# The feed-forward part of two token chunks computed with seven block products in place of eight

## Chip, cores and metric

One core of a Trainium2 chip runs the whole kernel. The metric is the device time of one execution in microseconds (us); lower is better.

## What is computed

A trunk layer over 1152 tokens (128 context tokens and 1024 latent tokens), width D = 1024: four mixers, an output projection, a gated feed-forward part with a width-3 convolution, and a final norm. What the change touches is the last stretch:

```
h = rmsnorm(x, p['norm2_g']) * (1.0 + sc2) + sh2
z = h @ p['ffn_w_up']                      # 1024 -> 2 x 2816
zc = conv_w[0] * z[t-1] + conv_w[1] * z[t] + conv_w[2] * z[t+1] + conv_b
a, b = jnp.split(zc, 2, axis=-1)           # in rows of 64 tokens (latent)
x = x + g2 * ((gelu(a) * b) @ p['ffn_w_down'])   # 2816 -> 1024
y = rmsnorm(x, final_norm_g)
```

Everything is float32.

## The kernel before

Activations lie transposed: features on the 128 partitions, tokens along the free side, in three chunks c = 0, 1, 2 of 384 tokens (`CH`). Chunk 0 holds the 128 context tokens and 256 latent ones, chunks 1 and 2 latent tokens alone. A float32 product is made of three matmuls on split operands (`mm3`, L216): each weight tile and each activation tile is held as a rounded part (`hi`) and the rest (`lo`), and hi·hi, hi·lo and lo·hi are added up in PSUM (L219 to L221). Splitting costs a cast on ScalarE (ACT) and a subtraction on VectorE (DVE) or GpSimd (POOL): `load_split` (L201) does it for weights of 128x1024 with the subtraction on POOL (L213), `put_hl` (L269) for activations.

The order of the instructions on TensorE (PE) and on the SP queue, which issues nearly all loads, is that of the program; the other engines' orders are laid out by the compiler's scheduler, each engine then running its list strictly in order. Buffers are tiles of pools with a fixed number of slots: three raw weight tiles, four `whi`/`wlo` pairs, eight PSUM banks (three `psg`, five `psx`). A load waits for its slot.

The output projection (`wout`, L1412) adds its products to the residual `acc[c]` in SBUF (`acc_add`, L1393), takes squares on ACT (L1429), and `norm2` (L1448) makes from them the normed and split input `h2[c]` of the feed-forward part: sums over partitions on PE (`stats`, L223, L229), a root on ACT and a reciprocal on DVE, a broadcast by PE (`bcast`, L256, L266), then `ada_apply` (L283; L289 on DVE, L278 and L294 on ACT, L275 and L279 for the `lo` parts).

The feed-forward part (`ffn`, L1533) goes over 22 column blocks f of 128. `ffn_up` (L1487) loads the block's weights for a and for b and does for each chunk 8 x 3 matmuls each (`gemm`, L556), the convolution (`conv`, L1456: L1459 on ACT, two or four instructions L1461 on DVE), the gelu (L1472, ACT) and the product with b (L1480, POOL), and splits the result g (L1483, L1484); g never leaves SBUF. After every second block `ffn_down` (L1507) multiplies the two g tiles of each chunk by two row blocks of w_down, 8 output blocks of 6 matmuls each, and adds each onto `acc` (L1396, DVE). The first two blocks are interleaved by chunk (`ffn_up2`, L1493), so that the norm of chunk 2 has its place between the matmuls of chunks 0 and 1. The last `ffn_down` takes squares (L1519) and runs `final` (L1542) for each chunk: sums on PE (L1548), broadcast (L266), output tiles on DVE (L1565) and POOL (L1563), stores from the SP queue (L1566).

In all the feed-forward part has 22 x 3 x 48 = 3168 matmuls up and 22 x 3 x 24 = 1584 down, each of a 128x128 weight and 384 columns.

## Time and profile before

| what | us |
|---|---|
| time, median of 3 runs (lowest, highest) | 1466.95 (1464.58, 1469.35) |
| the profiled execution, its own time | 1465.13 |
| its span in the trace | 1463.2 |
| PE busy | 1400.9 (96%) |
| DVE, POOL, ACT busy | 744.8, 531.5, 506.8 |

The span is what the profiler saw, from the first to the last instruction; the time of the same execution is 1.9 us longer. A matmul's busy time overlaps that of its neighbours, so the pace of matmuls is read from how many start in a stretch.

### The profile page before, as it was taken

The page shows a single profiled execution, that of the slowest core. Times are in us where ns is not written, and L with a number is a line of the kernel's source. Part 1 is how long each engine was busy: PE and PEld are TensorE (multiplying, and loading weights), DVE is VectorE, ACT ScalarE, POOL GpSimd, SP SyncE. Part 2 cuts the span into 40 slices and gives each one's busy share as a digit, 9 for nine tenths or more (in the row PEclk, how much of TensorE's full clock was granted, in tenths as well). Part 3 has the DMA queues.
Part 4 walks back from the last instruction along what each step waited for, and adds up shares of the span by engine and source line. Part 5 has one row for each costly group of instructions (what it writes and reads, how often), then busy time and mean ns, then how long its engine had stood idle before and what let it go on. Part 6 is the DMA issues. An engine that isn't in the chain of part 4 may idle for free.

```text
span 1463.2 us, 24504 instructions
## 1 busy us (share of the span) xinstructions
PE 1400.9 (96%) x9852; PEld 1330.1 (91%) x9852; DVE 744.8 (51%) x1571; ACT 506.8 (35%) x910; POOL 531.5 (36%) x500
## 2 busy tenths in 40 slices
PE   5999989898999999999999999999999999999996
PEld 2898778776898799999999999999999999999996
DVE  7797464544756411654444444535353535353545
ACT  6533212445456321653231313131313131313134
POOL 2243696644415233633231313132322222223224
...
GB/s 346 158 147 260 277 215 231 127 179 123 100 166 149 221 22 37 58 30 58 44 44 42 33 43 44 43 44 44 43 44 44 30 46 28 57 30 58 15 1 129
DMA packets 167602, 139.36 MB, mean 95 GB/s; under 512 B 19393, under 2 KB 156993, under 8 KB 167489
## 3 DMA queue, kind: packets, MB, share of 16 engines
...
## 4 chain that ended last, share of the span: by engine, by line
PE 78%; DMA 6%; POOL 5%; DVE 5%; issue 3%; ACT 2%; ACTq 0%; SPq 0%; POOLq 0%; DVEq 0%
PE psg L219 17%; PE psg L220 17%; PE psg L221 17%; PE psx L219 6%; PE psx L221 6%; PE psx L220 6%; DMA gv_s<-t_ev 1%; PE psx L229 1%; DMA raw<-w_in 1%; DMA raw<-w_ada 1%; PE psx L746 1%; PE psx L266 1%; POOL wlo L213 1%; DVE Gt L1323 1%; PE psg L593 1%
## 5 line engine op out<-in xcount | busy, mean ns | idle before, releaser
L219 PE MATMUL psg<-hm,whi 128*128 128x384 f32 x1560 | 538.6, 345 | 1.3 <-ACT hm L278 1.3
L220 PE MATMUL psg<-hm,whi 128*128 128x384 f32 x1560 | 530.4, 340 | 2.7 <-POOL hm L275 2.7
L221 PE MATMUL psg<-hm,wlo 128*128 128x384 f32 x1560 | 529.7, 340 | 1.1 <-POOL wlo L213 1.1
L213 POOL TENSOR_TENSOR wlo<-raw,whi 128x1024 fp32r<-128x1024 f32 x88 | 223.3, 2544 | 458.8 <-ACT whi L209 458.8
L219 PEld LDWEIGHTS psg<-hm,whi 128*128 128x128 f32 x1560 | 295.2, 189 | 10.6 <-issue 7.7
L220 PEld LDWEIGHTS psg<-hm,whi 128*128 128x128 f32 x1560 | 295.2, 189 | 4.8 <-POOL hm L275 3.4
L221 PEld LDWEIGHTS psg<-hm,wlo 128*128 128x128 f32 x1560 | 295.2, 189 | 1.4 <-POOL wlo L213 1.4
L1396 DVE SCALAR_TENSOR_TENSOR acc<-psx,mod,acc 128x384 f32<-128x384 f32 (+1 forms) x352 | 170.5, 514 | 83.3 <-PE psx L221 83.2
L209 ACT CAST whi<-raw 128x1024 fp32r<-128x1024 f32 x92 | 95.4, 1049 | 263.1 <-PE psx L220 193.9
L219 PE MATMUL psx<-ghi,whi 128*128 128x384 f32 x528 | 177.7, 337 | 0.0
L220 PE MATMUL psx<-glo,whi 128*128 128x384 f32 x528 | 177.4, 336 | 0.0
L221 PE MATMUL psx<-ghi,wlo 128*128 128x384 f32 x528 | 177.3, 336 | 0.0
L1461 DVE SCALAR_TENSOR_TENSOR t_ga<-psg,vecs,t_ga 128x378 f32<-128x378 f32 (+1 forms) x176 | 88.2, 511 | 170.5 <-ACT t_ga L1459 167.3
L1461 DVE SCALAR_TENSOR_TENSOR t_gb<-psg,vecs,t_gb 128x378 f32<-128x378 f32 (+1 forms) x176 | 87.9, 510 | 75.3 <-ACT t_gb L1459 72.6
L1480 POOL TENSOR_TENSOR t_gb<-t_gb,t_ga 128x384 f32<-128x384 f32 x66 | 67.5, 1022 | 150.1 <-DVE t_gb L1461 144.3
L219 PEld LDWEIGHTS psx<-ghi,whi 128*128 128x128 f32 x528 | 100.0, 189 | 0.0
L220 PEld LDWEIGHTS psx<-glo,whi 128*128 128x128 f32 x528 | 99.8, 189 | 0.0
L221 PEld LDWEIGHTS psx<-ghi,wlo 128*128 128x128 f32 x528 | 99.8, 189 | 0.0
L1483 ACT CAST ghi<-t_gb 128x384 fp32r<-128x384 f32 x66 | 33.9, 513 | 180.9 <-POOL t_gb L1480 180.9
L1484 DVE TENSOR_TENSOR glo<-t_gb,ghi 128x384 fp32r<-128x384 f32 x66 | 36.9, 559 | 109.6 <-ACT ghi L1483 109.6
L1472 ACT ACTIVATE t_ga<-t_ga 128x384 f32<-128x384 f32 x66 | 34.7, 526 | 95.4 <-DVE t_ga L1461 95.4
L1459 ACT ACTIVATE t_ga<-psg,vecs 128x384 f32<-128x384 f32 x66 | 44.2, 670 | 50.8 <-PE psg L221 50.8
...
## 6 DMA issues: line engine op xcount, KB each, us to landing
...
```

Source lines behind the costliest of these rows:

```text
L209: nc.scalar.copy(hi[:, :w], raw[:, :w])
L213: e.tensor_tensor(out=lo[:, :w], in0=raw[:, :w], in1=hi[:, :w].bitcast(F32), op=ALU.subtract)
L219: nc.tensor.matmul(ps, wh, ah, start=first and k == 0, stop=False)
L220: nc.tensor.matmul(ps, wh, al, start=False, stop=False)
L221: nc.tensor.matmul(ps, wl, ah, start=False, stop=last and k == nk - 1)
L1396: self.nc.vector.scalar_tensor_tensor(out=x, in0=ps[:, s0:s1], scalar=self.mod[:, sect + m, j:j + 1], in1=x, op0=ALU.mult, op1=ALU.add)
L1459: nc.scalar.activation(t, ps, AF.Identity, bias=self.vec("cb", f, 1), scale=w(1))
L1461: stt = lambda o, i, j: V.scalar_tensor_tensor(out=o, in0=i, scalar=w(j), in1=o, op0=ALU.mult, op1=ALU.add)
L1472: self.nc.scalar.activation(t, t, AF.Gelu_apprx_tanh)
L1480: G.tensor_tensor(out=t, in0=t, in1=ga, op=ALU.mult)
L1483: nc.scalar.copy(hi, t)
L1484: V.tensor_tensor(out=lo, in0=t, in1=hi.bitcast(F32), op=ALU.subtract)
```

## The change

Chunks 1 and 2 (768 tokens) together are treated as a product of 2x2 block matrices by a form of Strassen's scheme. Up: the four quarters of the input are features 0-511 and 512-1023 of chunk 1 and of chunk 2; the four quarters of the weights for one f are the two feature halves of its a block and of its b block. Seven products of sums of quarters (`hB[1]` to `hB[7]` with a, b and the sums P and Q), of 4 x 3 matmuls each, take the place of eight. Chunk 0 is computed as before. Down: the quarters are rows 0-1407 and 1408-2815 of w_down by its two column halves, and g of blocks f < 11 and f >= 11 by chunk; seven products of 11 x 4 x 3 matmuls take the place of eight.

The pieces, by the names in the diff:

- `wout` also writes each piece of the residual `acc` to DRAM (`x_s`), from the ACT queue. `norm2(2)` and `h_sums` now come ahead of the feed-forward part; `h_sums` makes the sums of quarters in place in `acc[1]` and `acc[2]` and splits them. The pool `zb`, opened by `open_zb`, lies where these two `acc` tiles were, and holds the weight sums (tag S), the g tiles and others.
- `ffn_up` handles one f at a time: per f on PE p1 (12 matmuls), three (36), a for chunk 0 (24), p2 (12), p43 (24), b for chunk 0 (24). `up_w` loads and sums weights; a and Q are split with DVE, b and P with POOL. `up_tail` finishes the outputs of chunks 1 and 2. `store` writes g to DRAM (`GV_s`; `G0_s` for chunk 0), for f >= 11 with four differences made on POOL (`tsub`), all by the ACT queue.
- `ffn_down` runs after all of up: first chunk 0 in all eight PSUM banks (22 steps of 24 matmuls), while the sums of w_down are made (S1 to S4 in SBUF), then the products 1, 6, 2, 7, 5, 4, 3, each in four banks (11 steps of 12 matmuls). g is loaded from DRAM and split again, step by step (`gload`); products 1, 2 and 4 load quarters of w_down again. The residual comes back by `xin` into two slots, and `final` of chunks 0 and 1 runs inside products 1 and 3.

```diff
                     def f(ps):
                         self.acc_add(c, m, ps, 16)
+                        self.nc.scalar.dma_start(self.x_s[c, :, m], self.acc[c][:, m])
...
-    def norm2(self, c, pool):
-        r = self.stats(self.sqs[c], 3, 1.0 / D, pool)
+    def norm2(self, c, zs):
+        r = self.stats(self.sqs[c], 3, 1.0 / D, zs)
         yield
         xs = [self.acc[c][:, i] for i in range(KT)]
         pb = self.bcast(r, 3)
-        self.h2.append(self.ada_apply(xs, c, self.A2, self.mod[:, 24:32, :], pool, pb))
+        if c == 0:
+            self.h2 = self.ada_apply(xs, c, self.A2, self.mod[:, 24:32, :], self.shared, pb)
+            yield
+            return
+        for k in (0, 4, 1, 5, 2, 6, 3, 7):
+            self.nc.vector.scalar_tensor_tensor(out=xs[k], in0=xs[k], scalar=self.A2[:, k, 1:2], in1=pb, op0=ALU.mult, op1=ALU.mult)
+            self.nc.scalar.activation(xs[k], xs[k], AF.Identity, bias=self.mod[:, 24 + k, 1:2])
+        if c == 1:
+            self.hB = {v: [None] * 4 for v in range(1, 8)}
+            for k in range(4):
+                self.hB[1][k] = self.put_hl(1, xs[k])
+                self.hB[2][k] = self.put_hl(1, xs[k + 4], None, "pool")
         yield
+    def h_sums(self, ext):
+        V = self.nc.vector
+        ex = lambda: ext.tile([P, CH], F32R, tag="e", name="he", bufs=24)
...
+        for k in range(4):
+            b11, b21 = self.acc[1][:, k], self.acc[1][:, k + 4]
+            b12, b22 = self.acc[2][:, k], self.acc[2][:, k + 4]
+            self.hB[3][k] = split(b22, (self.hm(2), self.hm(2)), G)
+            tt(b11, b12, b11)
+            tt(b12, b22, b12)
+            tt(b22, b22, b11)
+            tt(b21, b21, b22)
+            self.hB[6][k] = split(b22, (ex(), ex()), V)
+            self.hB[7][k] = split(b12, (ex(), ex()), G)
+            self.hB[5][k] = split(b11, (self.hm(2), self.hm(2)), V)
+            self.hB[4][k] = split(b21, (ex(), ex()), G)
...
+        def sums():
+            p = sp().tile([P, 1024], F32, tag="S", name="s24", bufs=2)
+            q = sp().tile([P, 1024], F32, tag="S", name="s31", bufs=2)
+            V.tensor_tensor(out=q[:, hi], in0=b[:, lo], in1=b[:, hi], op=ALU.add)
+            V.tensor_tensor(out=q[:, lo], in0=a[:, lo], in1=b[:, lo], op=ALU.subtract)
+            V.tensor_tensor(out=p[:, lo], in0=q[:, hi], in1=a[:, lo], op=ALU.subtract)
+            V.tensor_tensor(out=p[:, hi], in0=a[:, hi], in1=p[:, lo], op=ALU.subtract)
+            return p, q
+        return lambda: split(a, V), lambda: split(b, G), sums, split
...
+    def mmq(self, ps, w, o, v, first=True):
+        for i in range(4):
+            x = slice(o + i * P, o + (i + 1) * P)
+            self.mm3(ps, (w[0][:, x], w[1][:, x]), self.hB[v][i], i, 4, first, True, not first)
...
+    def zt(self, tag):
+        pool, n = {"p1": ("zs", 2), "X": ("zs", 2), "T": ("zs", 2), "gb": ("zb", 7), "Y": ("zb", 1), "c": ("zb", 2)}[tag]
+        return getattr(self, pool).tile([P, CH], F32, tag=tag, name="z" + tag, bufs=n)
...
+    def up_tail(self, f, ps, ga, X, Y, C22):
+        tt = lambda o, x, y: self.nc.vector.tensor_tensor(out=o, in0=x, in1=y, op=ALU.add)
+        self.gs[f, 2] = [C22, None]
+        c21 = self.zt("c")
+        tt(c21, ps[7], X)
+        g1 = self.up_gb(c21, 1, f, ga[1])
+        c12 = self.zt("c")
+        tt(c12, ps[5], X)
+        ga[2] = self.up_ga(c12, 2, f)
+        g2 = self.up_gb(C22, 2, f, ga[2])
+        self.store(f, g1, g2)
...
+    def store(self, f, g1, g2):
...
+        put = lambda v, t: nc.scalar.dma_start(self.GV_s[v - 1, f % 11], t)
+        if f < 11:
+            put(1, g1)
+            self.gk = g1, g2
+            return
+        b11, b12 = self.gk
+        put(2, g1)
+        put(3, g2)
+        T = lambda x, y: self.tsub(x, y)
+        t1 = T(b12, b11)
+        put(5, t1)
+        t3 = T(g2, b12)
+        put(7, t3)
+        t2 = T(g2, t1)
+        put(6, t2)
+        put(4, T(g1, t2))
+
+    def tsub(self, x, y):
+        t = self.zt("T")
+        self.nc.gpsimd.tensor_tensor(out=t, in0=x, in1=y, op=ALU.subtract)
+        return t
...
+        fs = [f for j in range(11) for f in (j, j + 11)]
...
+        def p1(f, w):
+            x[f] = {1: self.psx(CH)}
+            self.mmq(x[f][1], w, 0, 1)
+            t = st[f] = self.zt("p1")
+            nc.scalar.copy(t, x[f][1])
+
+        def p2(f, w):
+            self.mmq(x[f][1], w, 512, 2, False)
+            return self.up_ga(x[f].pop(1), 1, f)
+
+        def three(f, p, q):
+            X = self.zt("X")
+            ps = self.psx(CH)
+            self.mmq(ps, p, 0, 6)
+            tt(X, ps, st.pop(f))
+            x[f][7] = self.psx(CH)
+            self.mmq(x[f][7], q, 0, 7)
+            Y = self.zt("Y")
+            tt(Y, x[f][7], X)
+            x[f][5] = self.psx(CH)
+            self.mmq(x[f][5], q, 512, 5)
+            tt(Y, x[f][5], Y)
+            return X, Y
+
+        def p43(f, b, p):
+            self.mmq(x[f][7], b, 512, 4, False)
+            self.mmq(x[f][5], p, 512, 3, False)
...
+        f, g = fs[0], fs[1]
+        wa, wb, sums, split = self.up_w(f, sp)
...
+        a, b = wa(), wb()
+        p1(f, a)
+        ga[f][0] = self.up_ga(self.gemm(a, self.h2), 0, f)
+        ga[f][1] = p2(f, a)
+        wa2, wb2, sums2, split = self.up_w(g, sp)
+        nb = self.gemm(b, self.h2)
+        a2 = wa2()
+        p1(g, a2)
+        ga[g][0] = self.up_ga(self.gemm(a2, self.h2), 0, g)
+        ga[g][1] = p2(g, a2)
+        self.open_zb()
+        self.up_gb(nb, 0, f, ga[f][0])
+        P_, Q_ = sums()
+        q, p = split(Q_, V), split(P_, nc.gpsimd)
+        X, Y = three(f, p, q)
+        p43(f, b, p)
+        self.up_tail(f, x[f], ga[f], X, None, Y)
+        P_, Q_ = sums2()
+        b2 = wb2()
+        q, p = split(Q_, V), split(P_, nc.gpsimd)
+        X, Y = three(g, p, q)
+        nb = self.gemm(b2, self.h2)
+        p43(g, b2, p)
+        self.up_gb(nb, 0, g, ga[g][0])
...
+        for f in fs[2:]:
+            wa, wb, sums, split = self.up_w(f, sp)
+            ga = {}
+            a = wa()
+            P_, Q_ = sums()
+            q, p = split(Q_, V), split(P_, nc.gpsimd)
+            b = wb()
+            p1(f, a)
+            X, Y = three(f, p, q)
+            ga[0] = self.up_ga(self.gemm(a, self.h2), 0, f)
+            ga[1] = p2(f, a)
+            p43(f, b, p)
+            nb = self.gemm(b, self.h2)
+            self.up_gb(nb, 0, f, ga[0])
+            self.up_tail(f, x[f], ga, X, None, Y)
...
+        def gload(src, e):
+            r = dn.tile([P, CH], F32, tag="gr", name="gr", bufs=3)
+            nc.sync.dma_start(r, src)
+            h = dn.tile([P, CH], F32R, tag="gh", name="gh", bufs=4)
+            l = dn.tile([P, CH], F32R, tag="gl", name="gl", bufs=4)
+            nc.scalar.copy(h, r)
+            e.tensor_tensor(out=l, in0=r, in1=h.bitcast(F32), op=ALU.subtract)
+            return h, l
+
+        g0 = [gload(self.G0_s[f], G) for f in (0, 11)]
...
+        def fin(c, m, src):
+            for s0, s1, j in SEG[c]:
+                t = acc[c][:, m, s0:s1]
+                V.scalar_tensor_tensor(out=t, in0=src[:, s0:s1], scalar=self.mod[:, 40 + m, j:j + 1], in1=t, op0=ALU.mult, op1=ALU.add)
+            q = dn.tile([P, CH], F32, tag="sq", name="sq", bufs=2) if sq.get(c) else dn.tile([P, CH], F32, tag="ss", name="ss", bufs=2)
+            nc.scalar.activation(q, acc[c][:, m], AF.Square)
+            if sq.get(c):
+                G.tensor_tensor(out=sq[c], in0=sq[c], in1=q, op=ALU.add)
+            else:
+                sq[c] = q
+        sq = {}
...
+            for i in range(KT):
+                y = dn.tile([P, CH], F32, tag="yo", name="yo", bufs=4)
+                V.scalar_tensor_tensor(out=y, in0=xs[i], scalar=self.vec("nf", i, 1), in1=pb, op0=ALU.mult, op1=ALU.mult)
+                nc.sync.dma_start(self.a["o_y"][i * P:(i + 1) * P, c * CH:(c + 1) * CH], y)
+            yield
...
+        def stream(nk, steps, ps, first, late=3, side=()):
+
+            n = len(ps)
+            held, side = [], dict(side)
+            for i, mk in enumerate(steps):
+                hi, lo, o, g = mk()
+                if i >= nk - late:
+                    held.append((i, hi, lo, o, g))
+                    continue
+                for m in range(n):
+                    x = slice(o + m * P, o + (m + 1) * P)
+                    self.mm3(ps[m], (hi[:, x], lo[:, x]), g, i, nk, first, True, not first)
+                if i in side:
+                    side[i]()
+            for m in range(n):
+                for i, hi, lo, o, g in held:
+                    x = slice(o + m * P, o + (m + 1) * P)
+                    self.mm3(ps[m], (hi[:, x], lo[:, x]), g, i, nk, first, True, not first)
+                yield m
...
+                    s1, s2, s3, s4 = s
+                    V.tensor_tensor(out=s1, in0=ra[:, hi], in1=rb[:, hi], op=ALU.add)
+                    V.tensor_tensor(out=s3, in0=ra[:, lo], in1=ra[:, hi], op=ALU.subtract)
+                    V.tensor_tensor(out=s2, in0=s1, in1=ra[:, lo], op=ALU.subtract)
+                    V.tensor_tensor(out=s4, in0=rb[:, lo], in1=s2, op=ALU.subtract)
+                    return h, l, 0, g
...
+                        hl[k // 2] = wsplit(x, n * 512, V if k % 4 else G)
+                    h, l = hl[k // 2]
+                    return h, l, k % 2 * 512, gload(self.GV_s[v - 1, k], V if k % 2 else G)
+                yield mk
+        A_, B_ = B[0:4], B[4:8]
+        for m in stream(22, n0_steps(), B, True, 3, {6: lambda: xin(0)}):
+            fin(0, m, B[m])
+        f0 = final(0, (B_[0], B_[1]))
+        xin(1)
+        for m in stream(11, p_steps(1, (0, 0)), A_, True, 1, {4: lambda: next(f0), 7: lambda: next(f0)}):
+            nc.scalar.copy(X[:, m], A_[m])
+        next(f0)
+        for m in stream(11, p_steps(6, 2), B_, True, 1):
+            tt(X[:, m], B_[m], X[:, m])
+        xin(2)
+        for m in stream(11, p_steps(2, (11, 0)), A_, False, 1):
+            fin(1, m, A_[m])
+        for m in stream(11, p_steps(7, 3), B_, True, 1):
+            tt(Y[:, m], B_[m], X[:, m])
+        for m in stream(11, p_steps(5, 1), A_, True, 1):
+            tt(Y[:, m], A_[m], Y[:, m])
+            fin(2, m + 4, Y[:, m])
+        for m in stream(11, p_steps(4, (11, 512)), B_, False, 1):
+            tt(Y[:, m], B_[m], X[:, m])
+            fin(1, m + 4, Y[:, m])
+        f1 = final(1, (B_[0], B_[1]))
+        for m in stream(11, p_steps(3, 4), A_, False, 3, {4: lambda: next(f1), 7: lambda: next(f1)}):
+            tt(X[:, m], A_[m], X[:, m])
+            fin(2, m, X[:, m])
+        next(f1)
+        for _ in final(2, (B_[2], B_[3])):
+            pass
...
+        n = k.norm2(2, k.zs)
+        next(n), next(n)
         L.close()
-        ff = k.ffp = L.open("ff")
-        L.close(4)
-        R.close()
+        k.h_sums(L.open("ext"))
+
+        def open_zb():
+            R.close()
+            k.zb = R.open("zb")
+        k.open_zb = open_zb
+        k.ffn_up()
+        L.close(2)
+        R.close(3)
+        k.ffn_down(L.open("dn"))
+        L.close(2)
```

## Rows read from the trace of the kernel before

**Rows 1.** The page: span, busy time and chain shares by engine.
```profile
span 1463.2 us, 24504 instructions
...
PE 1400.9 (96%) x9852; PEld 1330.1 (91%) x9852; DVE 744.8 (51%) x1571; ACT 506.8 (35%) x910; POOL 531.5 (36%) x500
...
PE 78%; DMA 6%; POOL 5%; DVE 5%; issue 3%; ACT 2%; ACTq 0%; SPq 0%; POOLq 0%; DVEq 0%
```
**Rows 2.** Windows: stretch, us, busy (and count) by engine, PE clock, DMA share, GB/s.
```profile
700.00:800.00 100.00, 100.00 (x574) 100.00 (x573) 43.94 (x87) 25.97 (x38) 25.58 (x15) 1.00 0.15 43
...
1427.90:1449.80 21.90, 19.94 (x103) 18.97 (x102) 15.18 (x29) 13.96 (x28) 10.93 (x12) 0.84 0.26 95
1435.00:1440.00 5.00, 5.00 (x23) 5.00 (x22) 4.25 (x8) 3.31 (x7) 2.74 (x3) 0.72 0.77 281
```
**Rows 3.** Timeline (start, us, instruction), TensorE, last token chunk.
```profile
1427.57 0.34 PE L221 MATMUL psx<-ghi,wlo 128*128 128x384 f32 x1
1428.82 0.83 PE L1548 MATMUL psg<-ones,t_sq 128*128 128x1 f32 x6 [0.92 <-POOL t_sq L1524]
...
1431.60 1.65 PE L266 MATMUL psg<-ident,r 128*128 128x128 f32 x6 [0.79 <-DVE r L238]
...
1434.00 0.52 PE L219 MATMUL psx<-ghi,whi 128*128 128x384 f32 x1
1434.32 0.52 PE L220 MATMUL psx<-glo,whi 128*128 128x384 f32 x1
...
1449.45 0.34 PE L221 MATMUL psx<-ghi,wlo 128*128 128x384 f32 x1
```
**Rows 4.** Timeline, all engines, end of the output projection, up to 612 us.
```profile
596.63 1.39 PE L229 MATMUL psx<-ones,ss 128*128 128x1 f32 x12
...
602.19 0.83 PE L266 MATMUL psx<-ident,r 128*128 128x128 f32 x6
...
603.33 2.41 POOL L213 TENSOR_TENSOR wlo<-raw,whi 128x1024 fp32r<-128x1024 f32 x1 [1.09 <-ACT whi L209]
...
604.71 1.45 DVE L279 SCALAR_TENSOR_TENSOR hm<-tmp,mod,hm 128x384 fp32r<-128x384 f32 x1
...
605.70 1.33 POOL L1431 TENSOR_TENSOR ss<-ss,sq 128x384 f32<-128x384 f32 x1
...
609.44 0.60 DVE L1396 SCALAR_TENSOR_TENSOR acc<-psg,mod,acc 128x384 f32<-128x384 f32 x1
...
611.12 0.51 ACT L1429 ACTIVATE ss<-acc 128x384 f32<-128x384 f32 x1
```
**Rows 5.** Groups by form, 500 us to the end: busy, mean ns, idle before.
```profile
L209 ACT CAST whi<-raw 128x1024 fp32r<-128x1024 f32 x70 | 72.5, 1050 | 244.3 <-PE psx L220 193.9 <-PE psg L220 50.3
...
L1480 POOL TENSOR_TENSOR t_gb<-t_gb,t_ga 128x384 f32<-128x384 f32 x66 | 67.5, 1022 | 150.1 <-DVE t_gb L1461 144.3 <-DVE r L238 5.8
L1459 ACT ACTIVATE t_gb<-psg,vecs 128x384 f32<-128x384 f32 x66 | 44.2, 670 | 21.7 <-PE psg L221 19.4
...
L1484 DVE TENSOR_TENSOR glo<-t_gb,ghi 128x384 fp32r<-128x384 f32 x66 | 36.9, 559 | 109.6 <-ACT ghi L1483 109.6
...
L289 DVE SCALAR_TENSOR_TENSOR tmp<-acc,A,psx 128x384 f32<-128x384 f32 x8 | 4.6, 610 | 1.4 <-POOL hm L275 1.2
...
L279 DVE SCALAR_TENSOR_TENSOR hm<-tmp,mod,hm 128x384 fp32r<-128x384 f32 x4 | 4.3, 1087 | 0.0
...
L289 DVE SCALAR_TENSOR_TENSOR tmp<-acc,A,psx 128x256 f32<-128x256 f32 x8 | 3.8, 470 | 0.0
```
**Rows 6.** Waits (engine, line, waited for: us in total, times, longest): ACT.
```profile
ACT t_ev L1083 <- DMA gv_s<-t_ev: 19.1, 7, 3.7
```
**Rows 7.** Tile gv_s: its DMA issues, duration in ns, min/median/max.
```profile
L1082 ACTq DMA_DIRECT2D gv_s<-t_ev x9: 326/326/371, 292.2 to 344.5; - x9
```
**Rows 8.** Timeline, DVE and GpSimd, the last output tiles.
```profile
1455.88 2.71 DVE L1565 SCALAR_TENSOR_TENSOR yo<-acc,vecs,psg 128x384 f32<-128x384 f32 x5 [1.77 <-ACT rb L1559]
...
1455.92 2.91 POOL L1563 TENSOR_TENSOR yo<-yo,rb 128x384 f32<-128x384 f32 x3 [2.80 <-ACT rb L1559]
```

More of the change, by code (lines that the diff above doesn't have):

```diff
@@ L214, in load_split, with mm3 @@
         return hi, lo
-    def mm3(self, ps, whl, ahl, k, nk, first=True, last=True):
+    def mm3(self, ps, whl, ahl, k, nk, first=True, last=True, cont=False):
         nc = self.nc
         (wh, wl), (ah, al) = whl, ahl
-        nc.tensor.matmul(ps, wh, ah, start=first and k == 0, stop=False)
-        nc.tensor.matmul(ps, wh, al, start=False, stop=False)
-        nc.tensor.matmul(ps, wl, ah, start=False, stop=last and k == nk - 1)
+        nc.tensor.matmul(ps, wh, ah, start=first and k == 0, stop=False, skip_group_check=cont)
+        nc.tensor.matmul(ps, wh, al, start=False, stop=False, skip_group_check=cont)
+        nc.tensor.matmul(ps, wl, ah, start=False, stop=last and k == nk - 1, skip_group_check=cont)
     def stats(self, sqs, nt, inv_d, pool, heads=False):
@@ L1466, in conv, with up_w, split, up_ga @@
             stt(t[:, 63:64], ps[:, 64:65], 2)
-    def up_a(self, f, c, w, pool):
-        ps = self.gemm(w, self.h2[c])
-        t = self.tmp(pool, "ga", 4)
+    def up_w(self, f, sp):
+        nc, V, G = self.nc, self.nc.vector, self.nc.gpsimd
+        raw = []
+        for o in (0, DFF):
+            t = self.rp.tile([P, 1024], F32, tag="raw", name="raw", bufs=self.rawn)
+            nc.sync.dma_start(t.rearrange("p (k m) -> p k m", k=KT),
+                              self.a["w_up"][:, o + f * P:o + (f + 1) * P].rearrange("(k p) m -> p k m", p=P))
+            raw.append(t)
+        a, b = raw
+        lo, hi = slice(0, 512), slice(512, 1024)
+        def split(x, e):
+            h = self.rp.tile([P, 1024], F32R, tag="whi", name="whi", bufs=4)
+            l = self.rp.tile([P, 1024], F32R, tag="wlo", name="wlo", bufs=4)
+            nc.scalar.copy(h, x)
+            e.tensor_tensor(out=l, in0=x, in1=h.bitcast(F32), op=ALU.subtract)
+            return h, l
[15 more added lines that the diff above has]
+        return getattr(self, pool).tile([P, CH], F32, tag=tag, name="z" + tag, bufs=n)
+    def up_ga(self, ps, c, f):
+        t = self.tmp(self.shared, "ga", 5)
         self.conv(ps, c, f, t)
@@ L1487, in ffn_up @@
-    def ffn_up(self, f, pool):
-        w = self.w_cols("w_up", f * P)
-        ga = [self.up_a(f, c, w, pool) for c in range(NCH)]
-        w = self.w_cols("w_up", DFF + f * P)
-        return [self.up_b(f, c, w, ga[c], pool) for c in range(NCH)]
-    def ffn_up2(self, pool, n2):
-        w = [(self.w_cols("w_up", f * P), self.w_cols("w_up", DFF + f * P)) for f in range(2)]
-        out = [[], []]
-        for c in range(NCH):
-            for f in range(2):
-                ga = self.up_a(f, c, w[f][0], pool)
-                if (c, f) == (1, 0):
-                    next(n)
-                out[f].append(self.up_b(f, c, w[f][1], ga, pool))
-                if (c, f) == (0, 1):
-                    n = self.norm2(2, n2)
-                    next(n)
-        return out
@@ L1507, in ffn_down @@
-    def ffn_down(self, f0, gs, end=None):
-        w = [self.load_split(self.a["w_down"][(f0 + i) * P:(f0 + i + 1) * P, :]) for i in range(2)]
-        for c in range(NCH):
-            sq = []
-            for m in range(KT):
-                ps = self.psx(CH)
-                o = slice(m * P, (m + 1) * P)
-                for i in range(2):
-                    self.mm3(ps, (w[i][0][:, o], w[i][1][:, o]), gs[i][c], i, 2)
-                self.acc_add(c, m, ps, 40)
-                if end:
-                    q = self.tmp(end, "sq", 2)
-                    self.nc.scalar.activation(q, self.acc[c][:, m], AF.Square)
-                    if m in ((0, 6, 7) if c == 2 else (0,)):
-                        sq.append(q)
-                    else:
-                        e = self.nc.vector if c == 2 or m in (3, 5, 6) else self.nc.gpsimd
-                        e.tensor_tensor(out=sq[0], in0=sq[0], in1=q, op=ALU.add)
-                if end and (c and m in (2, 3) or (c, m) in ((1, 4), (2, 7))):
-                    next(fin)
-            if end:
-                fin = self.final(c, end, sq)
-        if end:
-            for _ in fin:
-                pass
@@ new lines, in up_gb @@
+    def up_gb(self, ps, c, f, ga):
+        t = self.zt("gb")
+        self.conv(ps, c, NF + f, t)
+        self.nc.gpsimd.tensor_tensor(out=t, in0=t, in1=ga, op=ALU.mult)
+        if c == 0:
+            self.nc.scalar.dma_start(self.G0_s[f], t)
+        return t
[10 more added lines that the diff above has]
+        self.store(f, g1, g2)
```

141 lines of the change are left out of this document (83 added, 58 removed).

## Prediction

> **What bounds it now.** I read the page first: TensorE (PE) is busy for 96% of the span and holds 78% of the chain that ended last; DVE, ACT and POOL are busy for a third to a half [rows 1]. Since a matmul's busy time overlaps its neighbour's, I next read the pace from windows: in the feed-forward part 574 matmuls start in 100 us with PE never idle and the clock at 1.00, so 0.1742 us each [rows 2]. There nothing but the number of matmuls counts. The timeline shows the two ends of that part. It begins near 607.2: the broadcast ends at 603.02 and 24 matmuls of 0.1742 follow [rows 4]. Its last matmul ends at 1449.8 [rows 3]. Between 1427.9 and 1449.8 PE gives way to the norms of chunks 0 and 1: 103 records, of which 24 belong to sums and broadcasts, so 79 matmuls take 21.9 us where 13.8 would do; the granted clock falls to a mean of 0.84, and near 1434 matmuls start 0.32 apart, PE's 1.2 GHz level [rows 2, 3]. From 1449.8 to 1463.2 there are 13.4 us of tail.
>
> **Matmuls removed.** Per f 132 in place of 144 (48 for chunk 0, 7 x 12 for the products), so 264 less; down 528 + 7 x 132 = 1452 in place of 1584, so 132 less. 396 x 0.1742 = **-69.0**. This is certain as long as PE is fed; all else is what feeding it costs. The Trainium skill (TensorE: Matmul & The Clock Gate, Back-to-back issue gap) gives columns / 2.4 + 2.5 ns for an isolated matmul: 162.5 ns for 384 columns, and by that estimate -64.4. The trace differs (174.2 ns [rows 2]), and I go by the trace.
>
> **The old end.** The 21.9 - 13.8 = 8.1 us go, since `final` of chunks 0 and 1 now sits inside products 1 and 3 with its inputs long ready; PE still pays 0.83 for sums and 0.83 for a broadcast [rows 3, 4], twice 1.7: **-4.8**.
>
> **norm2(2) ahead of the feed-forward part.** Before, 96 matmuls of the first two blocks covered it. Now PE waits after the last projection matmul (607.2) for DVE's `acc` (done 610.04, since DVE still works off norm2(1)), ACT's square (done 611.63) [rows 4], the sums (half of 1.39), root, reciprocal (some 0.6) and broadcast 0.83: about 614. Some 2.2 of these 7 us are PE's own work that it did before too. Bounds: +1.7 if DVE served `acc` at once, +5 as in the rows; I take 4, and 1.5 for a clock dip as after 1431, where 15 matmuls cost 15 x 0.146 = 2.2 [rows 3]: **+5.5**.
>
> **Start of up.** From the broadcast (t = 0) PE has 120 matmuls, 20.9 us, before `three`, which needs P's split. P's sum lies in `zb`, over `acc[1]` and `acc[2]`, so it waits until `h_sums` is through. DVE first applies the norm (8 x 0.61 [rows 5], in step with ACT); then `h_sums` wants 24 DVE instructions of 0.56 and 12 of POOL at 1.02 [rows 5]. These do not run side by side: a DVE instruction with two SBUF inputs, begun at 604.71 while POOL worked until 605.74, took 1.45, and POOL's next took 1.33 in place of 1.02; the mean of that form was 1.09 [rows 4, 5], while the form that reads PSUM kept its 0.61. One after the other: 13.4 + 12.2 = 25.7. Then four sums of 512 columns (0.56 + 0.14 for 128 columns more [rows 5] = 0.70 each, 2.8), the casts of Q and P (2 x 1.05) and POOL's subtraction (2.41 [rows 4]). Serial: 2 + 25.7 + 2.8 + 2.1 + 2.4 + 0.3 = 35.3, PE waits 14.4. If DVE and POOL never met, DVE alone needs 4.9 + 13.4 and the end comes near 28: 7. I take 12, nearer to the serial rows because each POOL instruction here has DVE's between, plus 2.2 for the clock. The second f then finds its P slot free only when product 4 of the first is done, with a cast and a subtraction (3.5) in 2.1 us of cover: 2.5 (0 to 5). **+16.7**.
>
> **The other 20 blocks.** An f lasts 132 x 0.1742 = 23.0. DVE's two-input work: four sums 2.8, splits of a and Q 2 x 1.26, six convolutions now out of SBUF 3.7: 9.0. POOL: 2 x 2.41 + 3 x 1.02 = 7.9, with the differences of f >= 11 another 4.1. Serial 16.9 or 21.0, so they fit. ACT: four casts 4.2, nine activations at most 6.0, a copy 0.5, and seven DMA issues at 0.33 [rows 7], together 13. The tight hand-off is P: its slot is free after product 3 (at 18.8 of 23.0) and P is wanted 2.1 into the next f: 6.3 us for 1.05 + 2.41 plus one POOL product 1.02 ahead: 1.8 spare. ACT also holds the stores of differences, which wait for POOL, and casts queue behind them. I take **+2**, bounds 0 and 25 (a little over 1 each).
>
> **Up to down.** The last f's differences need a slot that a store must free; a DMA behind which ACT waited took 2.7 on average, 3.7 at most [rows 6]. So they end some 10 us after the last matmul of up, and the pool of down (S3, S4, `gl`) may lie over their tiles. Steps 0 and 1 cover 8.4. One bank also waits 1.4 for its convolution. **+5**, 1.4 to 14.
>
> **Products.** For 23.0 us each they need 11 g splits (DVE 5 x 0.56, POOL 6 x 1.02), weights (POOL 3 x 2.41, DVE 2.5 x 1.26), 19.3 serial, and where a chunk finishes four more of each (6.5), 25.8: over the 23.0, evened out by four slots of look-ahead. **+2**, 0 to 15. DMA: 0.5 MB of weights and 0.4 of g in 4.2 us is 219 GB/s; 281 was reached [rows 2]. On the SP queue product 6's first g stands behind chunk 0's eight output stores, of which the fifth waits for a slot: broadcast at 16.7 + 1.7, four outputs 2.4, the DMA 2.7 after the first, four more: near 24; then load 2.7, cast 0.5, POOL 1.0: 28.3, and PE wants it at 24.7: 4, and 1.5 for the clock: **+5.5**, 0 to 7.
>
> **Tail.** After the last matmul: sum 0.56, `acc` 0.61, square 0.5, POOL 1.0, sums, root, reciprocal, broadcast some 2.5 with hand-overs, eight outputs on DVE alone with four slots 5.0, then the 4.4 from the last output (1458.83) to the end [rows 8]: 14.0 against 13.4, **+0.6** (-2 to +3).
>
> **Sum.** -69.0 - 4.8 + 5.5 + 16.7 + 2 + 5 + 2 + 5.5 + 0.6 = -36.5. The profiled execution took 1465.13, 1.8 under the median of the runs shown: 1428.6, and I say **1428**.
>
> **Rivals.**
> *All hand-offs covered.* For it: the three helper engines are idle for half the time [rows 1], and the scheduler may place the chains better than I did. Against it: `zb` on top of `acc`. Only the lower bounds remain: -69.0 - 4.8 + 1.7 + 9 + 1.4 = -61.7: 1403. I give 0.25 to all below 1412.
> *DVE and POOL set the pace.* Place: the P split in every f and the splits in every product. For it: 1.45 and 1.33 in [rows 4]. If all 12 two-input DVE instructions of an f lost 0.48 (1.09 - 0.61), an f >= 11 would need 21.0 + 5.8 = 26.8, 3.8 over, and an f < 11 22.7, just within; a few hand-overs more and each f is late by 2, each product by 2.5: 44 + 18 in place of 4, so 1486, slower. Against it: the waits shorten where PE waits. It decides from 1.3 us for each of the 29 units (36.5 / 29). The Trainium skill (SBUF — State Buffer, Who interferes with whom) states the rule behind it, an exclusive lock between a two-input DVE instruction and POOL's reads; by that, the trace agrees in [rows 4]. I give 0.08 to over 1470 and 0.02 to 1461 to 1470.
> *Partly so*: half the lateness, 1440 to 1461: 0.15. My forecast, 1412 to 1440: 0.50.
>
> **Numbers.** A difference of 0.3% (4.4 us) is about what a measurement of this kernel can tell. Faster by more than that: 0.25 + 0.50 + 0.15 = 0.90; within 0.02; slower 0.08. The range leaves out these upper 0.10, a little of what is partly so, and some 0.05 below the first rival's 1403: 1402 to 1458.
>
> **What would show it.** Right: PE's count falls by 396; 120 matmuls after the broadcast, then an idle of 7 to 14 us that POOL's `wlo` ends; up at 23 us per f with PE busy; gaps of a few us where down begins and at product 6, the latter ended by a g load. Wrong: no gap after the 120 (the first rival), or PE idle in every f, released by POOL or DVE (the second); a gap ended by `gr` or `raw` in many steps would mean that DMA sets the pace, which I priced at nothing.

## The result: 2.4% slower, and the profile after

The changed kernel took 1501.76 us (median of 4 runs, 1499.04 to 1502.72), the kernel before 1465.76 beside it: a ratio of 1.0241, 95% interval 1.0214 to 1.0269. The forecast was 1428 with a range of 1402 to 1458. Where some runs of a kernel lie more than 1.5% above its fastest, the ratios here leave those out. First the page, to be read beside [rows 1]:

```profile
span 1497.2 us, 24611 instructions
...
PE 1363.3 (91%) x9444; PEld 1280.9 (86%) x9444; DVE 961.8 (64%) x1590; ACT 602.1 (40%) x1058; POOL 693.1 (46%) x616
...
PE 61%; issue 9%; POOL 9%; DMA 8%; DVE 8%; ACT 3%; SPq 1%; ACTq 0%; POOLq 0%; DVEq 0%
```

TensorE (PE) has 408 records less and is busy for 37.6 us less, yet the span is 34 us longer: PE waits now, which it hardly did before in this part. Where, the windows tell (columns as in [rows 2], the engines in the order PE, PE's weight loads, DVE, ACT, POOL). Each line is one stage: from chunk 2's sums of squares to the first product 6, from there to the product 6 of the fourth f, the other 19 f from there to the end of up, the start of the down projection, the rest of it, and the tail.

```profile
613.95:656.16 42.21, 25.62 (x133) 24.74 (x133) 37.08 (x59) 24.40 (x49) 23.63 (x17) 0.77 0.10 30
656.16:714.79 58.63, 54.15 (x288) 53.00 (x288) 42.63 (x54) 18.36 (x25) 23.87 (x14) 0.94 0.23 73
714.79:1184.73 469.94, 451.29 (x2495) 445.90 (x2496) 343.65 (x508) 176.36 (x265) 196.54 (x132) 0.98 0.23 75
1184.73:1203.60 18.87, 0.34 (x3) 0.02 (x2) 5.72 (x10) 3.79 (x7) 7.93 (x8) 0.62 0.43 146
1203.60:1480.34 276.74, 264.38 (x1476) 259.93 (x1476) 175.06 (x187) 119.52 (x189) 157.19 (x103) 0.97 0.49 163
1480.34:1497.20 16.86, 3.09 (x12) 2.71 (x12) 8.54 (x14) 1.31 (x3) 2.66 (x3) 0.58 0.36 129
```

The third row holds the largest loss: 2495 matmuls at the 0.1742 of [rows 2] are 434.6 us, and they took 469.9, 35.3 more. 18.7 us of that (469.9 less PE's busy 451.3) are idle time. In e4_store_pool below, where PE waits only once in this stage, the same matmuls keep it busy for 439.4 us: a pace of 0.176, 4.8 us more than the 0.1742 gives, for which no run here shows a reason. The remaining 11.9 us are matmuls at PE's lower clock level. The timeline of PE shows both kinds of loss at the start of an f, and the window behind it the granted clock, 0.50:

```profile
814.17 0.44 PE L214 MATMUL psx<-he,whi 128*128 128x384 f32 x1 [0.85 <-ACT whi L1513]
814.45 0.34 PE L215 MATMUL psx<-he,whi 128*128 128x384 f32 x1
816.60 0.45 PE L216 MATMUL psx<-he,wlo 128*128 128x384 f32 x1 [1.81 <-POOL wlo L1514]
...
817.49 0.52 PE L214 MATMUL psx<-he,whi 128*128 128x384 f32 x1
817.81 0.52 PE L215 MATMUL psx<-he,whi 128*128 128x384 f32 x1
```
```profile
817.49:820.00 2.51, 2.51 (x9) 2.51 (x9) 1.19 (x3) 1.83 (x3) 0.30 (x1) 0.50 0.00 0
```

PE reaches product 6, waits for the cast of P and then for its rest (GpSimd, POOL), 2.7 us in all, and soon after it some ten matmuls start 0.32 apart, the 1.2 GHz level of [rows 3]. Over the stage the waits cost some 1.6 times their length (18.7 + 11.9). A pair of f (one below 11, one from 11 on) lasts 49.6 us (eight of them from 766.94 to 1164.03) where 264 x 0.1742 = 46.0 would do. Why P comes late is told by ScalarE's (ACT's) queue ahead of it, with POOL below (start, us, instruction, idle before and what ended it; ACTq marks a DMA issue in ACT's queue, `zp` is the copy of product 1):

```profile
794.95 0.46 ACT L1600 COPY zp<-psx 128x384 f32<-128x384 f32 x1
798.40 0.33 ACTq L1564 DMA_DIRECT2D GV_s<-zgb  x1
799.68 0.35 ACTq L1547 DMA_DIRECT2D G_s<-zgb  x1
801.26 0.33 ACTq L1564 DMA_DIRECT2D GV_s<-zgb  x1
802.36 0.33 ACTq L1564 DMA_DIRECT2D GV_s<-zT  x1
802.73 1.05 ACT L1513 CAST whi<-raw 128x1024 fp32r<-128x1024 f32 x1 [7.32 <-PE psx L215]
805.94 1.42 ACTq L1564 DMA_DIRECT2D GV_s<-zT  x2
807.41 0.67 ACT L1490 ACTIVATE t_ga<-psg,vecs 128x384 f32<-128x384 f32 x1 [3.63 <-PE psx L216]
807.98 1.04 ACT L1513 CAST whi<-s 128x1024 fp32r<-128x1024 f32 x1
...
813.09 1.03 ACT L1513 CAST whi<-s 128x1024 fp32r<-128x1024 f32 x1
```
```profile
797.35 2.30 POOL L1545 TENSOR_TENSOR zgb<-zgb,t_ga 128x384 f32<-128x384 f32 x2 [1.59 <-issue]
800.20 1.03 POOL L1545 TENSOR_TENSOR zgb<-zgb,t_ga 128x384 f32<-128x384 f32 x1 [0.55 <-DMA GV_s<-zgb]
801.31 1.02 POOL L1583 TENSOR_TENSOR zT<-zgb 128x384 f32<-128x384 f32 x1
804.37 2.63 POOL L1583 TENSOR_TENSOR zT<-zgb,zT 128x384 f32<-128x384 f32 x2 [2.04 <-DMA GV_s<-zT]
```

Each store is issued the moment POOL has made what it stores (zT ends at 802.33, its store is issued at 802.36). ACT does nothing else from 795.4 to 802.7 although its next job, the cast of `a`, needs none of these results. In each of the 18 blocks from the fourth to the last but one this cast begins 7.7 to 7.9 us behind `zp`'s copy. The last of the three casts, P's, begins at 813.09. (The wait in front of the cast at 802.73 is put down to PE, which has to free its buffer too; e4_store_pool below shows how much of it is PE's.) Among the waits (us in total, times, longest) there was nothing like these before:

```profile
ACT whi L1513 <- POOL zT L1583: 72.6, 11, 7.4
...
ACT t_ga L1490 <- POOL zT L1583: 29.1, 7, 7.3
POOL zT L1583 <- DMA GV_s<-zT: 26.5, 11, 5.7
```

The second loss is at the start of down, where ACT's queue and POOL's read

```profile
1193.08 8.55 ACTq L1564 DMA_DIRECT2D GV_s<-zT  x3
1201.68 0.92 ACT L1691 CAST gh<-gr 128x384 fp32r<-128x384 f32 x2 [14.70 <-DMA GV_s<-zT]
```
```profile
1198.71 2.57 POOL L1583 TENSOR_TENSOR zT<-zgb,zT 128x384 f32<-128x384 f32 x2 [5.66 <-DMA GV_s<-zT]
```

with PE idle for 18.5 us until the first weights' cast: the casts of the first g and weights stand behind the last f's stores, and the third difference waits 5.66 for one of its two buffers to be stored. The third is in down, on SyncE's (SP's) queue:

```profile
1318.14 5.66 SPq L1723 DMA_DIRECT2D o_y<-yo  x8
1323.89 16.73 SPq L1688 DMA_DIRECT2D gr<-GV_s  x11
1340.67 0.43 SPq L1675 DMA_DIRECT2D acc<-x_s  x1
1341.15 0.43 SPq L1781 DMA_DIRECT2D raw<-w_down  x1
```

Product 6's loads of g stand behind the eight output stores, as predicted (PE 3.2 idle at 1326.97); but the loads of g have three buffers, each waits there for one, and the next weights wait behind all eleven and behind 1.5 MB of `x_s`.

### The profile page after: what moved, and what is told of

Its sections match the earlier page's. It is cut to its first block, busy times and chain, and to the rows that moved or that the text cites. A ratio compares the mean times of both kernels' runs of the same rounds, so it can differ in the third digit from the quotient of the medians.

```text
span 1497.2 us, 24611 instructions
## 1 busy us (share of the span) xinstructions
PE 1363.3 (91%) x9444; PEld 1280.9 (86%) x9444; DVE 961.8 (64%) x1590; ACT 602.1 (40%) x1058; POOL 693.1 (46%) x616
## 4 chain that ended last, share of the span: by engine, by line
PE 61%; issue 9%; POOL 9%; DMA 8%; DVE 8%; ACT 3%; SPq 1%; ACTq 0%; POOLq 0%; DVEq 0%
PE psx L216 9%; PE psg L214 9%; PE psx L215 9%; PE psx L214 8%; PE psg L215 8%; PE psg L216 8%; DMA raw<-w_in 2%; POOL wlo L1514 2%; DMA raw<-w_down 1%; PE psx L741 1%; PE psx L224 1%; DMA raw<-w_ada 1%; DMA hm<-xT 1%; PE psx L261 1%; PE psg L588 1%
## 5 line engine op out<-in xcount | busy, mean ns | idle before, releaser
L214 PE MATMUL psg<-hm,whi 128*128 128x384 f32 x856 | 300.5, 351 | 0.9 <-ACT hm L273 0.9
L215 PE MATMUL psg<-hm,whi 128*128 128x384 f32 x856 | 292.6, 342 | 2.7 <-POOL hm L270 2.7
L216 PE MATMUL psg<-hm,wlo 128*128 128x384 f32 x856 | 292.1, 341 | 2.2 <-POOL wlo L208 2.2
L214 PEld LDWEIGHTS psg<-hm,whi 128*128 128x128 f32 x856 | 163.0, 190 | 10.3 <-issue 7.4
L215 PEld LDWEIGHTS psg<-hm,whi 128*128 128x128 f32 x856 | 163.1, 191 | 4.8 <-POOL hm L270 3.4
L216 PEld LDWEIGHTS psg<-hm,wlo 128*128 128x128 f32 x856 | 162.9, 190 | 2.6 <-POOL wlo L208 2.6
L214 PE MATMUL psx<-hm,whi 128*128 128x384 f32 x376 | 128.5, 342 | 1.8 <-ACT zp L1600 1.8
L215 PE MATMUL psx<-hm,whi 128*128 128x384 f32 x376 | 128.0, 340 | 0.0
L216 PE MATMUL psx<-hm,wlo 128*128 128x384 f32 x376 | 128.0, 340 | 0.0
L214 PE MATMUL psx<-he,whi 128*128 128x384 f32 x264 | 94.5, 358 | 19.3 <-ACT whi L1513 19.3
L214 PE MATMUL psx<-gh,whi 128*128 128x384 f32 x286 | 97.2, 340 | 3.2 <-ACT gh L1691 3.2
L215 PE MATMUL psx<-gl,whi 128*128 128x384 f32 x286 | 97.5, 341 | 2.5 <-DVE gl L1692 2.1
L215 PE MATMUL psx<-he,whi 128*128 128x384 f32 x264 | 93.7, 355 | 0.0
L214 PE MATMUL psg<-gh,whi 128*128 128x384 f32 x198 | 67.9, 343 | 18.5 <-ACT whi L1682 18.5
L1514 POOL TENSOR_TENSOR wlo<-raw,whi 128x1024 fp32r<-128x1024 f32 x22 | 53.3, 2421 | 60.9 <-ACT whi L1513 60.9
```

The source lines that it names most:

```text
L214: nc.tensor.matmul(ps, wh, ah, start=first and k == 0, stop=False, skip_group_check=cont)
L215: nc.tensor.matmul(ps, wh, al, start=False, stop=False, skip_group_check=cont)
L216: nc.tensor.matmul(ps, wl, ah, start=False, stop=last and k == nk - 1, skip_group_check=cont)
L1514: e.tensor_tensor(out=l, in0=x, in1=h.bitcast(F32), op=ALU.subtract)
```

## Experiments

Three theories of the up stage. STORE: ACT's casts stand behind stores that wait for POOL. LOCK: VectorE (DVE) and POOL, which take turns, pace the work whatever ACT does. SLOT: P's cast gets the last of four `whi` buffers to be freed. The work up to chunk 2's sums, which no edit touches, ended between 611 and 631 us in these profiles, so single times are read with that in mind and stages by windows behind the sums. The kernel before took 1475 to 1479 us beside these runs and 1465.8 beside the changed kernel, so these times are not compared with the 1501.76 to the microsecond.

**e1_t4**
```diff
-"T": ("zs", 2)
+if tag == "T": return self.zs.tile([P, CH], F32, tag="ss", name="zT", bufs=4)
```


> Edit: the differences for product inputs (zT) get four buffers instead of two, in memory that is idle during the up projection. Theory STORE (ScalarE's queue holds the stores of g and of its differences, which wait for GpSimd, and the casts of the weights stand behind them): GpSimd's waits for a buffer's store (26.5 us over 11 waits) go, the last difference of an odd f comes 4 to 6 us earlier, the PE gap at the start of the down projection falls from 18.9 to about 13 us and each odd f loses about 2 us less: about 1475 us. Theory LOCK (VectorE's and GpSimd's two-input operations take turns, and these two engines pace the up projection whatever ScalarE does): only the 6 us at the start of down are won: about 1495. Theory SLOT (the operand P is late because its buffers are the last to be freed): the same 1495.

1493.8 us. A pair took 48.5 us (49.6). PE's idle at the start of down fell by 0.9 only, to 17.6: the difference's buffer was not the last thing there. The time is the one that LOCK and SLOT gave, but these put the gain at the start of down; it came in the 19 f (459.6 us in place of 469.9). So a small part of STORE, well short of its 1475.

**e2_p_first**
```diff
-q, p = split(Q_, V), split(P_, nc.gpsimd)
+p, q = split(P_, nc.gpsimd), split(Q_, V)
```


> Edit: in the loop over f the operand P is cast and split ahead of Q, so it takes the buffer that is freed earlier. Theory SLOT: P's cast starts about 4 us earlier, the PE waits at product 6 (one or two each f, 0.8 to 1.8 us) vanish, the up projection goes back to about 46 us per pair of f: about 1470 us. Theory STORE: P's cast still stands behind the stores that wait for GpSimd, and at most 10 us are won: 1490 or more. Theory LOCK: about 1500.

1491.9 us, a pair 48.9. PE's waits moved from P's rest to Q's (up to 2.0 us, eight times). SLOT falls as the main cause.

**e3_store_sp**
```diff
-self.nc.scalar.dma_start(self.G0_s[f], t)
+self.nc.sync.dma_start(self.G0_s[f], t)
-put = lambda v, t: nc.scalar.dma_start(...)
+put = lambda v, t: nc.sync.dma_start(...)
+nxt = self.up_w(fs[i + 3], sp)   # ahead of the block's last gemm
```


> Edit: the stores of g and of the differences are issued by SyncE instead of ScalarE, and the weight loads of a block are issued one block earlier, so that they don't stand behind those stores. Theory STORE: ScalarE no longer waits for GpSimd's products and differences, a pair of f takes about 46.5 us instead of 49.6 (some 31 us in all), the start of up about 4 us less; the gap at the start of down stays 15 to 19, since the loads of g stand behind the stores: about 1465 us. Theory LOCK: a pair still takes 48.5 us or more: 1490 or more. Theory SLOT: P's cast still waits for its buffer, a pair takes about 49: 1495.

1556.6 us, a pair 55.9: STORE's 1465 is missed by far. LOCK's words (48.5 or more, 1490 or more) hold, but not its cause: SP's queue and a line of the waits show where the time went:

```profile
862.69 1.49 SPq L1564 DMA_DIRECT2D GV_s<-zgb  x2
864.22 5.17 SPq L1564 DMA_DIRECT2D GV_s<-zT  x4
869.49 1.13 SPq L1504 DMA_DIRECT2D raw<-w_up  x2
```
```profile
ACT whi L1513 <- DMA raw<-w_up: 180.9, 20, 11.8
```

The weight loads now stand behind the waiting stores. Moving the wait to another in-order queue moved the damage; one block of lead did not cover it.

**e4_store_pool** (POOL issues the stores: `nc.gpsimd.dma_start` in both places of e3_store_sp, nothing else)

> Edit: the same stores are issued by GpSimd, which makes what they store. Theory STORE: the same relief for ScalarE as with SyncE, and no store is ever waited for by another queue, so the gap at the start of down falls below 15 us: 1455 to 1475. Theory LOCK: GpSimd is busier by the issues and paces the work more: 1500 or more. Theory SLOT: about 1495.

1469.2 us. The windows of the same six stages:

```profile
620.22:660.37 40.15, 25.91 (x132) 25.21 (x132) 36.25 (x59) 24.29 (x49) 21.55 (x17) 0.80 0.05 14
660.37:718.12 57.75, 53.28 (x289) 52.45 (x289) 44.71 (x56) 18.73 (x25) 30.80 (x25) 0.93 0.28 85
718.12:1158.56 440.44, 439.40 (x2497) 439.08 (x2496) 361.40 (x506) 177.62 (x264) 248.41 (x216) 1.00 0.26 83
1158.56:1175.66 17.10, 0.78 (x4) 0.20 (x3) 7.97 (x10) 5.52 (x8) 10.64 (x13) 0.64 0.19 69
1175.66:1450.67 275.01, 263.33 (x1475) 259.22 (x1475) 173.70 (x186) 117.63 (x187) 156.07 (x103) 0.98 0.50 164
1450.67:1467.40 16.73, 3.09 (x12) 2.71 (x12) 8.37 (x14) 1.31 (x3) 2.69 (x3) 0.58 0.37 130
```

Read the third row against the changed kernel's: 29.5 us less, PE idle for 1.0 us in all (one wait, at its first product), clock 1.00, while DVE and POOL have the same arithmetic and POOL 52 us more on its books (248 for 197, its issues). LOCK falls for this stage. The next cast after `zp`'s copy now comes as soon as PE frees its buffer:

```profile
791.21 0.46 ACT L1600 COPY zp<-psx 128x384 f32<-128x384 f32 x1
795.49 1.05 ACT L1513 CAST whi<-raw 128x1024 fp32r<-128x1024 f32 x1 [3.81 <-PE psx L215]
```

4.3 us behind the copy, in place of 7.8 (at most 4.3 in all 18 blocks). The start of down, expected below 15, gained little (17.1): its first split of g now stood behind the last differences on POOL.

**e10_const**
```diff
-self.nc.scalar.dma_start(self.G0_s[f], t)
+self.nc.scalar.dma_start(self.G0_s[f], self.h2[0][0].bitcast(F32))
 (the same source in put)
```


> Edit: the changed kernel with one difference: each store of g and of a difference, issued by ScalarE as often and as large as there, takes its data from a tile of h that has long been ready; so chunk 1's and 2's g, their differences and chunk 0's g reach the down projection with other contents (this part of the computation is left out), and ScalarE waits for none of GpSimd's results. Theory STORE: a pair of f takes 46 to 47 us instead of 49.6. If what costs is the issue of 9 to 10 stores per pair on ScalarE or their traffic, and not the waiting: 48.5 or more. Theory LOCK or SLOT: 49.

1452.4 us. The stage of 19 f, and the stores of chunks 1 and 2 in ACT's queue:

```profile
704.52:1145.52 441.00, 439.40 (x2496) 439.07 (x2496) 348.41 (x509) 177.74 (x265) 211.14 (x132) 1.00 0.20 63
```
```profile
L1564 ACTq DMA_DIRECT2D GV_s<-hm x77: 326/457/1478, 591.7 to 741.7; - x77
```

Within 0.6 us the time of e4_store_pool, with all stores issued by ACT. But nothing holds them here, so the scheduler put all of them ahead of 742: 61 of the 99 (chunk 0's among them) come before this stage, the other 38 in its first 37 us. For those 37 us issue and traffic, denser than in the changed kernel (84 stores in the stage), cost PE at most one wait of 1.6 us; the rest of the stage has no store at all. So this run alone does not part the waiting from the issue. The rows of the changed kernel do: four issues of 0.33 right behind the copy would have been over before 797, and PE frees the cast's buffer 4.3 us behind the copy; and in e4_store_pool the traffic is all there. That the 29 us are waiting is argued from these rows; that they come from the place of the stores in ACT's queue is shown by e4_store_pool, and again by e7_all and e8_all_act. (A second difference of e10_const, that POOL's buffers are free at once, is not needed: in e4_store_pool POOL waits 27.5 us for them in this stage.) The first stage, too, is 35.1 us here in place of 42.2.

**e6_hs_dve**
```diff
 def h_sums(self, ext):
-    G = self.nc.gpsimd
+    G = V
```


> Edit: the changed kernel with one difference: the 12 splits of the sums of h that GpSimd does go to VectorE, which then does all 36 operations there (24 before). Theory LOCK (in this stretch VectorE's two-input operations take 1.37 us while GpSimd works, 0.55 alone): the sums end about 4 us earlier although VectorE has half as much again to do, and the PE wait of 14.7 us before the first product 6 falls to 8 to 12; 1490 to 1500 us in all. Theory COUNT (VectorE is slow there by the number of its operations): they end 5 us or more later, the wait grows to 18 to 22, and the time with it.

1502.4 us, above the range by its late sums (622.7); behind them the first stage took 37.2 us, 5.0 less, and PE's wait 11.0. One form of DVE in the changed kernel and here (ns: min/median/max, first and last start):

```profile
L1470 DVE TENSOR_TENSOR hm<-acc,hm x4: 552/1358/1371, 625.4 to 638.2; 128x384 fp32r<-128x384 f32 x4
```
```profile
L1470 DVE TENSOR_TENSOR hm<-acc,hm x8: 553/558/559, 632.8 to 647.6; 128x384 fp32r<-128x384 f32 x8
```

Alone, DVE does 36 operations in 19.3 us; with POOL, 24 of them and POOL's 12 took 22.0. LOCK holds here. The Trainium skill (SBUF — State Buffer, Who interferes with whom) calls the shared port pair an exclusive lock; these rows agree.

**e5_down** (on e4_store_pool)
```diff
+acc[0] = dn.tile(...)            # allocated ahead of S1 to S4
-g0 = [gload(self.G0_s[f], G) for f in (0, 11)]
+g0 = [gload(self.G0_s[f], V) for f in (0, 11)]
-gr: bufs=3, loaded where it is split
+gr: bufs=6, loaded three ahead
-w_down: loaded where it is split
+w_down: loaded one pair ahead
-xin(2)                           # ahead of product 2
+for m in stream(11, p_steps(7, 3), B_, True, 1, {1: lambda: xin(2)}):
```


> Edit: as e4_store_pool (1469.2 us, its PE gaps at the start of the down projection 4.1 + 12.6 us, in the rest of it some 14 us), and in the down projection: the buffers of the weight sums S1 to S4 lie clear of the memory of the last g and differences, the first two splits of g go to VectorE, loads of g run three ahead in six buffers, loads of weights one pair ahead, x of chunk 2 is loaded during product 7. Theory A (each of these gaps is a transfer or a split that stands behind something unrelated in one in-order queue): the start gap falls to 5 to 8 in all, the gaps within down to 2 to 4: 1448 to 1453 us. Theory B (the transfers themselves or GpSimd's and VectorE's speed set the down projection): the gaps move to other places and at most 8 us are won: 1461 or more.

1469.7 us with the sums at 631.0, 10.8 later than in e4_store_pool; behind them 10.2 us less. The time is B's; of A the half within down came true: PE idle there is 3 us now, and 1474 matmuls take 261.5 us (276.7 for 1476 in the changed kernel). The start did not gain, it waits 18 us (16 in e4_store_pool): `gl` lies over the differences, and its split on DVE waited 11.7 us for a difference's store.

**e7_all and e8_all_act**
```diff
 h_sums as e6_hs_dve, differences as e1_t4, down as e5_down, and for the first f
+p, q = split(P_, V), split(Q_, V)
 self.up_gb(nb, 0, f, ga[f][0])
-q, p = split(Q_, V), split(P_, nc.gpsimd)
```


> Edit: e5_down and e6_hs_dve together, with four buffers for the differences as in e1_t4, and at the start of up the sums, casts and splits of P and Q of the first f (both splits by VectorE) ahead of chunk 0's product with its gate. If the four places are independent, the gains add: start of up 8 us less than in e4_store_pool (PE waits of 13.0 + 4.0 there), up at 46.4 us per pair of f as there, start of down 5 us in all, down 2 to 4: 1438 to 1445 us. If what one gives back turns up as a wait of the next stage: 1452 or more.

> Edit: e7_all with the stores of g and of the differences issued by ScalarE again, as in the changed kernel. Theory STORE: the pair of f goes from 46.4 back to 48.5 (as in e1_t4, with four buffers too) and the start of down waits some 5 us more: 22 to 30 us above e7_all. Theory LOCK or SLOT: within 8 us of e7_all.

e7_all 1452.3, e8_all_act 1474.6. The pairs: 46.5 and 48.5, as expected; the start of up waits the same 9.5 + 1.0 us in both, since the product that held P's cast is behind it now. Of the 22.3 us between the two, 3.9 lie ahead of the sums; the 19 f take 459.7 against 439.1, 20.6 more with nothing changed but the engine that issues the stores, while the start of down, where 5 us more had been expected, takes 3 less. e7_all missed its range by the start of down: 21.7 us idle, because six buffers of g lay over the four buffers of the differences, and all loads of g and the weights behind them left SP only at 1162.36.

**e9_best**
```diff
 e7_all without e1_t4's part, and
+ahead(4)                         # g's loads first: memory idle during up
 acc[0] = dn.tile(...)
 g0 = [gload(self.G0_s[f], V) for f in (0, 11)]
-{4: lambda: next(f1), 7: lambda: next(f1)}
+{i: lambda: next(f1) for i in (3, 5, 7)}
```


> Edit: e7_all (1452 us) with two buffers for the differences again; in the down projection the buffers are laid out so that the loads of g take memory that is idle during up and x's accumulator lies over the differences (in e7_all the loads of g waited at SyncE until 1162 us for memory that the last differences held, 22.0 us of PE idle); chunk 1's output is scaled two steps earlier, ahead of the last product's results. Theory A (the start of down waits for memory and queue places alone): the PE idle at the start of down falls from 22.0 to 7 to 10 us, the wait ahead of the last sums from 5.1 to 3.5 us: 1436 to 1442 us, some 2.5 per cent below the kernel before. Theory B (the last f's products and differences on GpSimd are needed by the first block of down): 15 us or more stay, 1446 or more.

1435.8 us (median of the four runs that the ratio uses, 1427.9 to 1439.5; 1438.7 over all six), ratio to the kernel before 0.9727, 95% interval 0.9678 to 0.9776. Its start of down and what follows:

```profile
1142.30:1153.15 10.85, 1.71 (x4) 0.59 (x4) 9.68 (x12) 6.34 (x10) 6.46 (x8) 0.62 0.15 54
1153.15:1417.55 264.40, 259.14 (x1474) 256.16 (x1474) 191.46 (x188) 116.38 (x186) 162.60 (x106) 0.99 0.52 173
1417.55:1431.90 14.35, 2.63 (x12) 2.25 (x12) 5.76 (x11) 1.16 (x3) 3.01 (x3) 0.63 0.31 110
```

Idle at the start is 9.1 us (4.54 + 1.11 + 3.49), at the last sums 3.2.

**e11_store_pool**

> The kernel of e4_store_pool (one difference to the changed kernel: GpSimd issues the stores of g and of the differences), timed in five rounds. In its first profile all that stands behind chunk 2's sums of squares took 36 us less than in the changed kernel, and the same work ahead of them 6 us more. Theory STORE: the 36 us are the store waits' and come back in every run: 1458 to 1470 us, a ratio of 0.988 to 0.998 to the kernel before. If the first look was a chance: 1475 or more, not faster than before.

1467.1 us (median of 12), ratio 0.9936, 95% interval 0.9905 to 0.9968; the kernel before took 1478.8 (median of 17) beside it. The queue of its stores alone, two lines of the changed kernel, decides between 2.4% slower than before and nearly the same (0.6% faster).

## Why the prediction was wrong, step by step

The steps of the sum against the changed kernel's windows:

| step | predicted, us | measured, us | over |
|---|---|---|---|
| from the broadcast to P's rest (616.3 to 658.6) | 20.9 + 12 + 2.2 = 35.1 | 42.3 | 7.2 |
| from there to the fourth f's product 6 (286 matmuls, to 714.8) | 49.8 + 2.5 = 52.3 | 56.2 | 3.9 |
| the other 19 f from there | 434.6 + 2 = 436.6 | 469.9 | 33.3 |
| up to down | 5 | 18.9 | 13.9 |
| products and four norm steps | 252.9 + 3.3 + 7.5 = 263.7 | 276.7 | 13.0 |
| tail | 14.0 | 16.9 | 2.9 |

Together 74.2 over. The profiled execution, 1499.04, stood 70.4 above the sum; the difference of 3.8 is in the work ahead of the sums and in small losses of the kernel before that the sum had kept.

- **Matmuls removed**: right. PE's count fell by 408 records (396), and where almost nothing waits (e4_store_pool) 2496 matmuls go at 0.176, 1% slower than the 0.1742 of the sum.
- **The old end** and **norm2(2) ahead**: right. No gap over 0.6 us at the norms of chunks 0 and 1; the sums waited 2.1 for ACT's square.
- **The other 20 blocks, +2**: the step that failed. It named the tight hand-off and the cause ("ACT also holds the stores of differences, which wait for POOL, and casts queue behind them"), then put it at +2 without a sum; what it did reckon of ACT was its total, 13 us in 23. What counts is not how much ACT has to do but how long the head of its queue waits: the cast of `a` came 7.8 us behind `zp`'s copy, 4.3 without the stores' waits. These 3.5 us are twice the 1.8 that P had to spare: P's cast came 18.1 us behind the copy, 15.0 in e10_const. So the wait that the prediction priced at +2 measured 29 to 29.5 (the changed kernel against e10_const and e4_store_pool). The bounds left out the clock, which gave the 18.7 us of idle another 11.9, and the pace, another 4.8.
- **Up to down, +5 (to 14)**: the cause was seen (a difference waits for its store), the size was short: 18.9. The step let the chain run beside the first blocks of down, but ACT's casts for these blocks are behind the same stores. With the stores' waits gone (e10_const) 13.0 are left, and 10.9 in e9_best.
- **Start of up, +16.7**: that the 36 operations of `h_sums` do not run side by side was right (22.0 us, where the serial reckoning has 25.7 and DVE's 24 alone 13.4; e6_hs_dve), and PE's wait lay at its upper bound (14.1, then 1.4 for the rest of P). On top of it, P's cast waited 4.13 us behind the store of chunk 0's g, which POOL's multiply, 4.22 us beside DVE's operations, delayed. That store the prediction did not place.
- **Products, +7.5**: product 6 as predicted (3.2 idle, ended by the load of g). The rest was priced as DVE's and POOL's time, but it was the loads' order and buffers: loads of weights behind loads of g that wait for three buffers. With loads ahead in six buffers it comes to 261.5 to 264.4, the predicted 263.7.
- **Tail**: 2.9 more, since chunk 1's outputs on DVE stood between the last product's; e9_best took 14.35.
- **The rivals**: "DVE and POOL set the pace" gave 1486, nearest to the result, but for a reason that e4_store_pool refutes for the 19 f. The rival that was missing, an in-order queue whose head waits, decides in the same place.

The size of the gain was there to be had, though not with this kernel: e9_best, which moves the stores, the splits of `h_sums`, the loads and the buffers, stands 2.7% below the kernel before, where the forecast stood 2.5% below. It is no proof of the sum: from the broadcast on e9_best takes 816 us, where the steps above have 806.7. What stays open is the rest of the start of up, where PE still waits 9.5 us in e9_best, ended by the cast of P, and the 10.9 us at the start of down.
